# A three-pass fp32 encoder trunk with a seven-product block scheme on one core: six units instead of four lead each FFN, the second rows' squares move ahead of a weight conversion, and 276 GpSimd sums and products are issued on VectorE

## The chip, the cores and the metric

The kernel runs on one core of a Trainium2 chip. A core has five engines that run at the same time, each through its own queue of instructions in order: TensorE (PE in the profile; its weight loads are PEld), VectorE (DVE), ScalarE (ACT), GpSimd (POOL) and SyncE (SP), which here starts most of the transfers. They meet through semaphores. Matmuls write the accumulators in PSUM; everything else stands in SBUF. Times are device microseconds (us) of one execution. The kernel before was run three times: 2573.06, 2574.07 and 2575.15 us, median 2574.07.

## The reference, cut to what matters

One layer (DEPTH = 1) over 2048 frames of 1024 channels, all in fp32:

```python
xn = rmsnorm(x, norm1_g)
z = xn @ w_in                          # 4608 columns
u_pool, zq, zf, zi, zo, zg = split(z)  # 512 each, and 2048 of gates
gates = sigmoid(zg + b_gate)
ya = pool_mixer(u_pool, ...) @ w_pa    # running means over 2, 4, 8 and 16 frames
yb = hgrn2_mixer(zq, zf, zi, zo, ...) @ w_pb
x = x + (gates[0] * ya + gates[1] * yb) @ w_o
h = rmsnorm(x, norm2_g) @ w_up         # 2 * 2816 columns
val, gate = split(causal_conv3(h) + conv_b)
x = x + (silu(gate) * val) @ w_down
return rmsnorm(x, final_g)
```

## The kernel before, in words

**Products.** Each large matrix product is cut two by two, in rows (frames), in columns and in the contracted channels, and is made of seven smaller products P1 to P7 instead of eight, in Strassen's manner. For that the activations are needed in seven *forms*: the blocks B11, B21 and B22 as they are, and the combinations T1 to T4 (P1 takes B11, P2 B21, P6 T2, P5 T1, P7 T3, P4 T4, P3 B22). The weights are needed in seven forms as well: P1, P2 and P4 take a quarter of the weights as it is, P5, P6, P7 and P3 a sum of two to four quarters. Each operand is then split into a rounded part (`h`) and the remainder (`l`), and each product is three matmuls: high by high, high by low, low by high. The results of P1, P6, P7 and so on are joined through three PSUM banks, X (P1, P2), Z (P6, P7, P4) and V (P5, P3), with copies and differences `e1`, `u2` and `u3` between them: ScalarE copies X to `e1` after P1, VectorE makes `u2` after P6 and `u3` after P7, each from Z and `e1`, and Z is free for the next product after that.

**Two halves.** The program goes twice through the same stages, once for each 1024 frames (blocks 0 and 1, then 2 and 3, of 512 frames each). A half is: the io projection (`proj_io`, values `v` and output gates `z`; here the frames stand on the partitions, with four column blocks `j` of each bank), the mixer (`mixer`: 14 units in the order of PROJ, with the heads' recurrence and the pooling as tasks between them), the two branches `pa` and `pb`, the output rows `wo`, and the FFN (`ffn`: 22 `up` units, then the rows `dn`, then the last norm).

**The weight stream.** `Stream` loads 512-column quarters into a ring of eight places (`raw`) and converts them into a ring of six operands (`ops`), at most four ahead of the product that uses them: `convert` has ScalarE copy the rounded part (line 205) and VectorE subtract it for the remainder (line 206). Where an operand is a sum, its conversion first makes the sum: three for an io P3, two for P6, one each for P5 and P7 (line 338, `w24s0` and so on; one sum of P6 and one of P3 stand on VectorE, the other 20 in all on GpSimd), and four per unit of the other projections (`comb`, line 397, on GpSimd, 56). This happens in the first half only; sums are kept in DRAM and loaded by the second half. The sums for `up`, `wo` and `dn` are made by accumulating transfers ahead of their use.

**The forms.** `forms_a_task` makes B11 and B21 of the first block of a half, `forms_b_task` the rest from the second block. Both begin with the row norms (`row_rstd`: two squares per row tile on ScalarE, line 635; GpSimd's scalar work; the scaling, line 649). Block 1's rows come through the task `nxt[2]`, and in the first half its steps are taken when the planner's slots come. T4, and T3 of the FFN's input, are differences of two SBUF tiles (lines 746 and 729, on GpSimd). `add_forms` (line 1103) makes the forms of `y` for the branches and of the gated FFN result `g` for `dn`, 120 sums, on GpSimd. GpSimd also has products by sigmoids (lines 1137, 1212, 1420, 1484) and the sums of two of the four pooling windows (line 778).

**What sets the order.** A scheduler that simulates the program's timeline lays the instructions on the engines' queues; `behind`, `second` and `in_turn` add order that has no data in it. `up_order` fixes the order of the `up` units' products: P1 and P2 of the heads, which need only block 0's forms B11 and B21, stand first; the other five products of the heads follow, and then unit by unit. With N_HEADS = 2 the heads are units 0 to 3.

```python
heads = [(0, 1), (2, 3), (4, 5)][:N_HEADS]
res = [(m, p) for ms in heads for p in ("P1", "P2") for m in ms]
```

## Time and profile before

| | before |
|---|---|
| median of three runs | 2574.07 us (2573.06 to 2575.15) |
| the profiled execution | 2575.64 us, its span 2573.9 us |
| mean granted TensorE clock | 0.993 of full speed |
| TensorE busy | 2519.3 us, 98% |
| VectorE busy | 1964.0 us, 76%, 3382 instructions |
| ScalarE busy | 1191.9 us, 46% |
| GpSimd busy | 851.5 us, 33%, 1209 instructions |

The span runs from the first to the last instruction; the execution's own time has 1.7 us around it. In the rows of the profile, `out<-in` gives the tiles by the program's names with the numbers left out, `x4` is a count, and the brackets at the end hold the idle time of the engine just before and what ended it. A row of waits gives the waiting engine, tile and line, then the releasing one, and total, count and longest. A row of a stretch of time gives its length, then busy us and count of PE, PEld, DVE, ACT and POOL, then the granted clock, the transfers' share and GB/s.

### The profile page before, as it was taken

How to read it: one execution, taken by the hardware profiler on the slowest of the kernel's cores; microseconds unless marked ns; L12 is line 12 of the kernel's file. 1: busy time of each engine (PE TensorE's matmuls, PEld its weight loads, DVE VectorE, ACT ScalarE, POOL GpSimd, SP SyncE). 2: the span in 40 equal slices, each digit the busy share in tenths (PEclk: the TensorE clock that was granted, in tenths of full speed). 3: DMA queues.
4: the chain of work that ended last, by engine and by line, in shares of the span. 5: the costliest groups of instructions: out<-in, count | busy, mean ns of one | idle time of the engine just before them, and what ended most of it. 6: DMA issues, size and time to landing. Idle time of an engine off the chain costs nothing.

```text
span 2573.9 us, 35491 instructions
## 1 busy us (share of the span) xinstructions
PE 2519.3 (98%) x11464; PEld 2057.0 (80%) x11464; DVE 1964.0 (76%) x3382; ACT 1191.9 (46%) x2244; POOL 851.5 (33%) x1209
## 2 busy tenths in 40 slices
PE   7899999999999999999999999999999999999998
PEld 6678888788788888878878888888887888888887
DVE  7878788478789777786486776775978987778844
ACT  5335434324555544554364354442355554445533
POOL 6534344031445333462141111200223433334502
PEclk9899999999999999999999999999999999999999
DMA  6787768767788888887364343356442454446942
GB/s 219 254 248 204 210 201 247 215 223 245 179 235 235 235 242 230 252 318 252 107 211 149 99 139 119 120 160 224 143 165 88 151 153 144 144 139 209 366 149 98
DMA packets 254058, 496.88 MB, mean 193 GB/s; under 512 B 26736, under 2 KB 43248, under 8 KB 253552
## 3 DMA queue, kind: packets, MB, share of 16 engines
q1 hardware_dynamic: 187968, 319.89, 38.5%
q0 software_dynamic: 41504, 110.64, 16.8%
q10 hardware_dynamic: 24400, 64.08, 7.3%
q8 instruction: 90, 1.47, 0.2%
q14 instruction: 96, 0.79, 0.1%
HBM read 384.94 MB, written 187.17 MB: 222 GB/s over the span
## 4 chain that ended last, share of the span: by engine, by line
PE 89%; DVE 5%; issue 2%; ACT 2%; DMA 1%; POOL 1%; SPq 0%; DVEq 0%; POOLq 0%; ACTq 0%
PE dn_P L145 16%; PE up_Z L145 14%; PE up_V L145 9%; PE up_X L145 9%; PE wo_P L145 6%; PE gr_Z L145 5%; PE pb L145 3%; PE pa L145 3%; PE gr_X L145 3%; PE gr_V L145 3%; PE fr_Z L145 3%; PE fr_V L145 2%; PE fr_X L145 2%; PE pl L867 1%; PE io_Z L145 1%
## 5 line engine op out<-in xcount | busy, mean ns | idle before, releaser
L205 ACT CAST ops<-raw 128x512 fp32r<-128x512 f32 x732 | 452.7, 620 | 792.9 <-PE dn_P L145 147.6
L206 DVE TENSOR_TENSOR ops<-raw,ops 128x512 fp32r<-128x512 f32 x732 | 555.4, 762 | 207.8 <-ACT ops L205 204.0
L1409 DVE SCALAR_TENSOR_TENSOR e<-h,cols,e 128x512 f32<-128x512 f32 x176 | 142.4, 812 | 30.8 <-ACT e L1407 26.5
L1407 ACT ACTIVATE e<-h,cols 128x512 f32<-128x512 f32 x176 | 142.4, 814 | 29.1 <-DVE h L997 21.0
L1412 DVE SCALAR_TENSOR_TENSOR e<-h,cols,e 128x512 f32<-128x512 f32 x176 | 133.7, 768 | 2.8
L805 POOL DMA_DIRECT2D g_P<-dg_P x154 | 83.3, 543 | 101.3 <-PE dn_P L145 28.5
L1103 POOL TENSOR_TENSOR gf_P<-e,e 128x512 f32<-128x512 f32 x44 | 65.6, 1493 | 153.3 <-DVE e L1418 98.8
L1103 POOL TENSOR_TENSOR gf_P<-gf_P,e 128x512 f32<-128x512 f32 x44 | 59.1, 1344 | 66.6 <-DVE e L1418 66.1
L1402 POOL COPY h<-h 128x2 f32<-128x2 f32 x88 | 39.5, 463 | 121.2 <-DVE h L995 119.2
L1404 POOL COPY hist<-h 128x2 f32<-128x2 f32 x88 | 38.8, 442 | 121.1 <-DVE h L997 119.4
L1416 ACT ACTIVATE e<-e 128x512 f32<-128x512 f32 x88 | 55.6, 632 | 46.2 <-DVE e L1412 46.0
L997 DVE TENSOR_TENSOR h<-up_u,up_V 128x512 f32<-128x512 f32 x88 | 60.0, 682 | 13.3 <-PE up_V L145 12.8
L1212 POOL TENSOR_TENSOR q<-q,qs 128x512 f32<-128x512 f32 x16 | 22.7, 1419 | 139.0 <-ACT qs L1211 127.9
L854 POOL COPY qm<-q 128x64 f32<-128x64 f32 x64 | 24.4, 404 | 117.7 <-DVE q L860 43.9
L1079 DVE TENSOR_TENSOR x<-x,wo_P 128x512 f32<-128x512 f32 x88 | 56.0, 675 | 8.3 <-PE wo_P L145 8.1
L1249 ACT ACTIVATE gt<-gt,cols 128x512 f32<-128x512 f32 x48 | 34.8, 725 | 57.5 <-DVE gt L997 35.1
L1079 DVE TENSOR_TENSOR ac<-ac,dn_P 128x512 f32<-128x512 f32 x72 | 47.3, 682 | 18.4 <-PE dn_P L145 16.5
L1103 POOL TENSOR_TENSOR yf_P<-ya,ya 128x512 f32<-128x512 f32 x16 | 21.1, 1322 | 117.3 <-DVE ya L1326 117.3
L628 POOL TENSOR_SCALAR ro<-so 128x4 f32<-128x4 f32 x16 | 3.2, 199 | 156.8 <-ACT junk L969 156.8
L1477 POOL TENSOR_TENSOR fss<-fss 128x1 f32<-128x1 f32 x16 | 6.6, 415 | 144.2 <-ACT fo L1467 144.2
L1432 POOL DMA_DIRECT2D dg_P<-gf_P x88 | 50.1, 569 | 8.5 <-POOL gf_P L1103 7.7
L1031 ACT COPY up_e<-up_X 128x512 f32<-128x512 f32 x44 | 25.8, 586 | 57.6 <-PE up_X L145 47.5
(1267 smaller groups left out, 8303.4 us busy)
## 6 DMA issues: line engine op xcount, KB each, us to landing
g_P<-dg_P POOLq DMA_DIRECT2D x154, 256.0 KB, 6.4
raw<-in_w_up_t SPq DMA_DIRECT2D x132, 256.0 KB, 3.1
raw<-in_w_in_t SPq DMA_DIRECT2D x98, 256.0 KB, 3.2
dg_P<-gf_P POOLq DMA_DIRECT2D x88, 256.0 KB, 3.8
raw<-in_w_io SPq DMA_DIRECT2D x68, 256.0 KB, 4.8
dg_P<-e SPq DMA_DIRECT2D x66, 256.0 KB, 3.2
raw<-in_w_dn SPq DMA_DIRECT2D x66, 256.0 KB, 4.5
x<-in_x SPq DMA_DIRECT2D x64, 256.0 KB, 5.1
```

The source lines that it names most:

```text
L145: count[1] = pe.matmul(*args, **kw)
L205: self.mark = act.copy(hi, v)
L206: dve.tensor_tensor(lo, v, f32(hi), ALU.subtract)
L805: eng.dma_start(t, d)
L997: dve.tensor_tensor(dst, t, ps, ALU.add if how == "add" else ALU.subtract)
L1079: dve.tensor_tensor(t, t, ps[j], ALU.add if sg > 0 else ALU.subtract)
L1103: pin(pool.tensor_tensor(t, x0, x1, op))
L1407: in_turn(act.activation(t, h[:, 2:], AF.Identity, bias=col(o_cb + mt), scale=col(o_cw + 4 * MF + mt)))
L1409: in_turn(second(dve.scalar_tensor_tensor(t, h[:, 1 : 1 + TB], col(o_cw + 2 * MF + mt), t, ALU.mult, ALU.add)))
L1412: dve.scalar_tensor_tensor(t, h[:, 0:TB], col(o_cw + mt), t, ALU.mult, ALU.add)
L1416: in_turn(act.activation(g, g, AF.Silu))
L1432: pool.dma_start(d, t)
```

## The change

Three things are edited. N_HEADS goes from 2 to 3, so P1 and P2 of units 4 and 5 join the leading products of each FFN. Right after block 0's forms are written out, one step of block 1's task is taken, which emits its row norms, and the first weight conversion from number 6 on is put behind the last of its squares (`opening`). And every `tensor_tensor` of two whole tiles that stood on GpSimd is issued on VectorE: 276 of them. Lines of the changed kernel are two to four numbers higher.

```diff
-N_HEADS = 2
+N_HEADS = 3
-G_POOL = 4
...
             self.mark = act.copy(hi, v)
+            if j >= N_OPS and opening[0] is not None:
+                behind(self.mark, opening[0])
+                opening[0] = None
             dve.tensor_tensor(lo, v, f32(hi), ALU.subtract)
...
-                        (dve if i == (p == "P6") and p != "P5" and p != "P7" else pool
-                         ).tensor_tensor(t2, t, r.tile, ALU.add)
+                        dve.tensor_tensor(t2, t, r.tile, ALU.add)
...
-            pool.tensor_tensor(t, x0, x1, ALU.add)
+            dve.tensor_tensor(t, x0, x1, ALU.add)
...
-        heads = [(0, 1), (2, 3), (4, 5)][:N_HEADS]
+        heads = [(0, 1), (2, 3), (4, 5), (6, 7)][:N_HEADS]
...
-            act.activation(junk[hf], halves[hf], AF.Square, accum_out=ss[:, hf : hf + 1])
+            ins = act.activation(junk[hf], halves[hf], AF.Square, accum_out=ss[:, hf : hf + 1])
+            if name == "x1_3":
+                opening[0] = ins
...
-                pool.tensor_tensor(t, full["B11"][k], t2, ALU.subtract)
+                dve.tensor_tensor(t, full["B11"][k], t2, ALU.subtract)
...
-            pool.tensor_tensor(t4, full["B21"][k], full["T2"][k], ALU.subtract)
+            dve.tensor_tensor(t4, full["B21"][k], full["T2"][k], ALU.subtract)
...
-        add = pool if g % 2 == 0 else dve
-            add.tensor_tensor(t[:, a:528], s[:, a:528], s[:, a - k : 528 - k], ALU.add)
+            dve.tensor_tensor(t[:, a:528], s[:, a:528], s[:, a - k : 528 - k], ALU.add)
...
-            pin(pool.tensor_tensor(t, x0, x1, op))
+            pin(dve.tensor_tensor(t, x0, x1, op))
...
-            (dve if hf == 0 else pool).tensor_tensor(t, t, g, ALU.mult)
+            dve.tensor_tensor(t, t, g, ALU.mult)
...
-                    pool.tensor_tensor(t, t, g, ALU.mult)
+                    dve.tensor_tensor(t, t, g, ALU.mult)
...
-                    (pool if m < G_POOL else dve).tensor_tensor(g, g, ts[0, hf], ALU.mult)
+                    dve.tensor_tensor(g, g, ts[0, hf], ALU.mult)
...
-                    pool.tensor_tensor(res[c], res[c], fg[c], ALU.mult)
+                    dve.tensor_tensor(res[c], res[c], fg[c], ALU.mult)
...
     join(nxt[1])
+    nxt[2].step()
     Task(setup_task())
```

What it does to the queues is shown at three places. The rows are the instructions in the order in which they stand on one engine.

ScalarE at the program's start, before. `raw6` to `ops6` is the seventh weight conversion, the lines of 663 are block 0's forms, those of 635 the squares of block 1's row tiles 0 to 3, and 1142 the copies of bank X after P1 (`io_e`).

```order
L205 CAST ops6_427<-raw6_110 128x512
L663 ACTIVATE x0_b6_268<-x0_t6_138,cols_84 128x512
L205 CAST ops7_444<-raw7_112 128x512
L663 ACTIVATE x0_b7_274<-x0_t7_139,cols_84 128x512
L635 ACTIVATE x1_xs0_0_307,x1_0ss_309<-x1_0_0_216 128x512
L635 ACTIVATE x1_xs0_1_308,x1_0ss_309<-x1_0_1_218 128x512
...
L635 ACTIVATE x1_xs3_1_341,x1_3ss_342<-x1_3_1_230 128x512
L1142 COPY io0_e1_0_449<-io0_X_0_290 128x512
L1142 COPY io0_e1_1_454<-io0_X_1_291 128x512
```

The same place with the change (lines 667, 637, 204 and 1145 are the same statements).

```order
L667 ACTIVATE x0_b6_268<-x0_t6_138,cols_84 128x512
L667 ACTIVATE x0_b7_274<-x0_t7_139,cols_84 128x512
L637 ACTIVATE x1_xs0_0_280,x1_0ss_282<-x1_0_0_216 128x512
L637 ACTIVATE x1_xs0_1_281,x1_0ss_282<-x1_0_1_218 128x512
...
L637 ACTIVATE x1_xs3_1_314,x1_3ss_315<-x1_3_1_230 128x512
L204 CAST ops6_427<-raw6_110 128x512
L204 CAST ops7_444<-raw7_112 128x512
L1145 COPY io0_e1_0_449<-io0_X_0_334 128x512
L1145 COPY io0_e1_1_454<-io0_X_1_335 128x512
```

Conversions 6 and 7 have moved from between block 0's last forms to behind the eight squares, right ahead of the copies.

VectorE toward the end of the io projection, before: `io0_u3` is read from bank Z after P7, `z0_1` is the output gate, `w24s0` the first of the three sums for the operand of conversion 24. The second and third sums (`w24s1`, `w24s2`) and the products of `z0_1` by their sigmoids stand on GpSimd.

```order
L1148 TENSOR_TENSOR io0_u3_3_1070<-io0_Z_3_710,io0_e1_3_470 128x512
L997 TENSOR_TENSOR z0_1_0_1072<-io0_u3_0_1055,io0_V_0_843 128x512
...
L997 TENSOR_TENSOR z0_1_3_1090<-io0_u3_3_1070,io0_V_3_846 128x512
L338 TENSOR_TENSOR w24s0_1099<-raw40_903,raw41_905 128x512
L338 TENSOR_TENSOR w25s0_1130<-raw44_962,raw45_999 128x512
L206 TENSOR_TENSOR ops24_1106<-w24s2_1103,ops24_1106 128x512
L338 TENSOR_TENSOR w26s0_1161<-raw48_1109,raw49_1111 128x512
L206 TENSOR_TENSOR ops25_1137<-w25s2_1134,ops25_1137 128x512
```

The same place with the change.

```order
L1151 TENSOR_TENSOR io0_u3_3_1070<-io0_Z_3_710,io0_e1_3_470 128x512
...
L1140 TENSOR_TENSOR z0_1_1_1078<-z0_1_1_1078,zs0_1_1_1079 128x512
L1000 TENSOR_TENSOR z0_1_3_1090<-io0_u3_3_1070,io0_V_3_846 128x512
L1140 TENSOR_TENSOR z0_1_2_1084<-z0_1_2_1084,zs0_1_2_1085 128x512
L340 TENSOR_TENSOR w24s0_1099<-raw40_903,raw41_905 128x512
L1140 TENSOR_TENSOR z0_1_3_1090<-z0_1_3_1090,zs0_1_3_1091 128x512
L340 TENSOR_TENSOR w24s1_1101<-w24s0_1099,raw42_934 128x512
L340 TENSOR_TENSOR w24s2_1103<-w24s1_1101,raw43_936 128x512
L340 TENSOR_TENSOR w25s0_1130<-raw44_962,raw45_999 128x512
L208 TENSOR_TENSOR ops24_1106<-w24s2_1103,ops24_1106 128x512
```

Between `io0_u3_3` and the remainder `ops24` there are now thirteen instructions instead of six: the four products and the chain `w24s0` to `w24s2` stand in VectorE's own queue, with two sums for the next operand among them.

ScalarE in the opening of the first FFN, before. `m1_T23h`, `m1_T10h` and so on are the rounded parts of the forms T2, T1 and T3, `h0_2` and `h0_3` the P2 results of units 2 and 3, `ops185` a weight conversion.

```order
L606 CAST m1_T23h_6787<-m1_t23_6783 128x512
L991 COPY h0_2_0_0_6794<-up0_2_X_6649 128x512
L606 CAST m1_T10h_6805<-m1_t10_6690 128x512
L991 COPY h0_3_0_0_6818<-up0_3_X_6669 128x512
L205 CAST ops185_6876<-raw171_6616 128x512
L606 CAST m1_T11h_6855<-m1_t11_6718 128x512
L205 CAST ops186_6895<-raw172_6635 128x512
L606 CAST m1_T12h_6864<-m1_t12_6753 128x512
```

The same place with the change.

```order
L608 CAST m1_T23h_6787<-m1_t23_6783 128x512
L204 CAST ops185_6867<-raw171_6616 128x512
L994 COPY h0_2_0_0_6794<-up0_2_X_6649 128x512
L608 CAST m1_T10h_6805<-m1_t10_6690 128x512
L994 COPY h0_3_0_0_6818<-up0_3_X_6669 128x512
L1034 COPY up0_4_e1_6838<-up0_4_X_6820 128x512
L608 CAST m1_T11h_6855<-m1_t11_6718 128x512
L204 CAST ops186_6887<-raw172_6635 128x512
L1034 COPY up0_5_e1_6862<-up0_5_X_6840 128x512
L994 COPY h0_4_0_0_6882<-up0_4_X_6820 128x512
L994 COPY h0_5_0_0_6901<-up0_5_X_6840 128x512
L608 CAST m1_T12h_6912<-m1_t12_6753 128x512
```

Four copies of units 4 and 5 (`up0_4_e1`, `up0_5_e1`, `h0_4`, `h0_5`) and their conversions stand among the casts of T1, all of them behind the last cast of T2, `m1_T23h`. On TensorE the groups of matmuls are the same; P1 and P2 of units 4 and 5 stand ahead of the first P6.

More of the change, by code (lines that the diff above doesn't have):

```diff
@@ L235, in tile_trunk @@
     urgent = [None]
+    opening = [None]
     def first(ins):
```

## The prediction, made blind

> **What bounds the kernel now.** I read the page first, then TensorE's waits, then the same work in the two halves of the program side by side, then the engines' timelines at the places found.
>
> ```profile
> span 2573.9 us, 35491 instructions
> ...
> PE 2519.3 (98%) x11464; PEld 2057.0 (80%) x11464; DVE 1964.0 (76%) x3382; ACT 1191.9 (46%) x2244; POOL 851.5 (33%) x1209
> ...
> PE 89%; DVE 5%; issue 2%; ACT 2%; DMA 1%; POOL 1%; SPq 0%; DVEq 0%; POOLq 0%; ACTq 0%
> ```
>
> TensorE is busy 98% of the span and carries 89% of the chain that ended last. The change touches no product, so all it can win is TensorE's idle time, 2573.9 - 2519.3 = 54.6 us, and time at a reduced clock. TensorE's own waits say where (total, times, longest, in us):
>
> ```profile
> PE x_t L655 <- DVE x_xs L649: 8.8, 2, 7.8
> PE fr_Z L145 <- DVE ops L206: 4.5, 1, 4.5
> PE io_Z L145 <- DVE io_u L1148: 4.3, 1, 4.3
> PE io_X L145 <- ACT io_e L1142: 3.5, 2, 3.0
> PE gr_Z L145 <- DVE gr_u L1033: 3.3, 2, 2.4
> PE up_Z L145 <- ACT m_T23h L606: 2.6, 2, 1.3
> PE up_Z L145 <- DVE m_T23l L607: 2.3, 2, 1.1
> PE up_Z L145 <- DVE up_u L1037: 2.2, 4, 0.6
> PE io_Z L145 <- DVE x_t L712: 2.1, 2, 1.8
> ```
>
> The 7.8 us is the program's first wait, for the first input rows; the change leaves it. The others lie in three places. In the next view (busy us and count by engine, clock, DMA share, GB/s) the first two rows are the io projection of the first and of the second half, the next two the rest of the mixer up to `pb`, then the openings of the two FFNs, then the rest of the first FFN's `up`:
>
> ```profile
> 16.90:113.70 96.80, 86.27 (x361) 68.83 (x362) 80.60 (x104) 43.17 (x84) 60.92 (x76) 0.93 0.65 219
> 1312.50:1395.20 82.70, 81.90 (x369) 66.60 (x370) 68.25 (x101) 44.52 (x86) 21.92 (x24) 1.00 0.48 158
> 113.70:524.30 410.60, 399.67 (x1977) 331.62 (x1976) 316.46 (x707) 167.16 (x368) 143.04 (x150) 0.99 0.76 220
> 1395.20:1787.60 392.40, 391.23 (x1970) 328.00 (x1969) 270.37 (x693) 166.60 (x363) 47.84 (x80) 1.00 0.44 139
> 650.70:712.00 61.30, 55.87 (x244) 43.40 (x244) 50.45 (x71) 33.27 (x63) 27.13 (x34) 0.97 0.77 188
> 1913.20:1974.50 61.30, 57.04 (x249) 44.53 (x248) 48.56 (x69) 34.26 (x63) 21.47 (x28) 0.97 0.28 87
> 712.00:1085.00 373.00, 373.00 (x1615) 302.73 (x1614) 305.54 (x429) 186.23 (x292) 156.91 (x224) 1.00 0.87 237
> ```
>
> The two halves multiply the same, but only the first makes the weights' sums (the second loads them). The first io pass is 14.1 us longer, the first mixer pass 18.2. An `up` opening idles 61.30 - 55.87 = 5.4 us, the second 4.3; the steady `up` idles not at all. Some waits also cost clock:
>
> ```profile
> 33.90:37.30 3.40, 3.40 (x10) 2.65 (x9) 2.40 (x2) 0.88 (x3) 3.17 (x7) 0.50 0.89 285
> 88.50:95.30 6.80, 5.22 (x12) 4.13 (x13) 6.80 (x12) 2.46 (x4) 2.17 (x2) 0.50 0.06 20
> 122.60:129.50 6.90, 5.02 (x12) 3.96 (x13) 4.58 (x9) 0.35 (x1) 0.00 (x0) 0.51 1.05 354
> 464.00:467.40 3.40, 3.40 (x10) 2.62 (x9) 2.52 (x5) 1.75 (x4) 0.00 (x0) 0.50 0.43 131
> 682.40:685.80 3.40, 3.40 (x9) 2.63 (x8) 3.39 (x2) 1.14 (x2) 3.40 (x4) 0.50 0.64 90
> 1945.30:1948.80 3.50, 3.50 (x11) 2.68 (x10) 2.88 (x3) 0.76 (x2) 3.50 (x3) 0.51 0.24 76
> ```
>
> After each of the long waits, and after the FFN openings' pairs of about 1.2 us, the granted clock is half; half of TensorE's busy time there is lost: 1.7, 2.6, 2.5, 1.7, 1.7 and 1.7 us. The account closes: the first io pass has 96.80 - 86.27 = 10.5 us of idling and 1.7 + 2.6 of clock, 14.8, for its 14.1.
>
> [...]
>
> **Part 1: the second rows' squares in front.** In the start, ScalarE waits 6.69 us for TensorE before the cast `ops6`, with the squares of block 1's rows queued behind it; they run 27.13 to 32.03 and hold up the copies `io_e`, for which TensorE waits:
>
> ```profile
> 24.93 0.62 ACT L205 CAST ops<-raw 128x512 fp32r<-128x512 f32 x1 [6.69 <-PE io_X L145]
> 27.13 0.63 ACT L635 ACTIVATE x_xs<-x 128x512 f32<-128x512 f32 x1
> 32.03 2.01 ACT L1142 COPY io_e<-io_X 128x512 f32<-128x512 f32 x4
> 32.74 0.71 PE L145 MATMUL io_X<-ops,x_f4h 128*128 128x512 f32 x2 [3.00 <-ACT io_e L1142]
> ```
>
> The new order puts the eight squares (4.9 us) into that hole of 6.69 us. The copies then follow the end of P1, 32.74 - 3.00 = 29.74, within one copy (2.01 / 4 = 0.5 us): 2.5 us of the wait goes, and its clock, 1.7. Block 1's forms start some 7 us earlier, so the waits for `x_xs` (8.8 - 7.8 = 1.0) and `x_t` (1.8) should shrink: I take 1.3 of 2.8. Gain **5.5**, bounds 3 and 2.5 + 1.7 + 2.8 = 7.
>
> **Part 2: 276 sums and products from GpSimd to VectorE.** By the code: 20 io sums, 56 of the other projections, 24 of the forms' differences, 16 pooling sums, 120 in the forms of `g` and `y`, 40 products. The same statement stood on both engines, which gives the price directly:
>
> ```profile
> L1420 DVE TENSOR_TENSOR e<-e,e 128x512 f32<-128x512 f32 x36 | 24.7, 686 | 0.6
> L1420 POOL TENSOR_TENSOR e<-e,e 128x512 f32<-128x512 f32 x8 | 10.6, 1327 | 24.9 <-ACT e L1416 24.9
> ```
>
> A sum lasts 0.69 us instead of 1.33, and a row of them advances by 2.47 / 4 = 0.62 us (the row at 89.26 below). So VectorE takes on 276 x 0.62 = 171 us of work. What it gives back is blocked time:
>
> ```profile
> 682.81 4.26 POOL L746 TENSOR_TENSOR m_t<-m_b,m_t 128x512 f32<-128x512 f32 x3
> 683.08 4.55 DVE L206 TENSOR_TENSOR ops<-raw,ops 128x512 fp32r<-128x512 f32 x1
> ...
> 75.28 6.88 POOL L746 TENSOR_TENSOR x_t<-x_b,x_t 128x512 f32<-128x512 f32 x4
> 89.26 2.47 DVE L1148 TENSOR_TENSOR io_u<-io_Z,io_e 128x512 f32<-128x512 f32 x4
> 93.13 5.92 POOL L1137 TENSOR_TENSOR z<-z,zs 128x512 f32<-128x512 f32 x4 [10.97 <-ACT zs L1136]
> 99.01 2.67 POOL L338 TENSOR_TENSOR w24s<-w24s,raw 128x512 f32<-128x512 f32 x2
> 101.71 0.62 ACT L205 CAST ops<-w24s 128x512 fp32r<-128x512 f32 x1 [6.88 <-POOL w24s L338]
> 102.36 1.12 DVE L206 TENSOR_TENSOR ops<-w24s,ops 128x512 fp32r<-128x512 f32 x1 [5.70 <-ACT ops L205]
> 113.30 1.31 DVE L206 TENSOR_TENSOR ops<-w27s,ops 128x512 fp32r<-128x512 f32 x1
> ```
>
> One VectorE subtraction with both inputs in SBUF lasted 4.55 us beside three GpSimd sums of 4.26; both engines crawl. The two mixer passes size it: the first has 56 sums more on GpSimd, and VectorE is busy 316.46 - 270.37 = 46.1 us longer, of which 14 more instructions explain 8.7. The other 37.4 / 56 = 0.67 us per sum is blocking. A moved sum costs VectorE 0.62 and frees 0.67: its load stays where it was. The gain is that a chain of sums gets twice as short.
>
> *The io pass.* From `io0_u3_0` to the last sum-made operand `ops27` VectorE needed 113.30 - 89.26 = 24.0 us; the new order has 30 instructions there, 30 x 0.62 = 18.6, against 4 + 3 products of 12 matmuls at 373.00 / 1615 = 0.231 us each in four column blocks, 7 x 2.77 = 19.4 us, on TensorE. So TensorE, not VectorE, should set the pace. To be won are 4.3, its clock 2.6 and some 0.9 of small waits, 7.8. The loads of four raw quarters for each of these operands stay, so I take **4.5**. Below: were nothing freed, 28 x 0.62 = 17.4 would join 80.60, 98 us in a stretch of 96.80, and 2 us would be lost.
>
> *The first mixer pass.* It opens with the 4.5 us for `ops` (clock 2.5), behind the `z` products of both engines; I take 5.5 of 7.0. Of the 2.4 us at 461 and its clock, 1.7, I take 2, and 1 goes back to new short waits: **6.5**, bounds 0 and 14 (all its idling, 10.9, and clock, 4.2, less the 1.2 that the second pass keeps).
>
> *Elsewhere* sums join VectorE where TensorE does not idle (`up`: 305.54 busy of 373.00, plus 48 x 0.62 = 30 if nothing is freed, still 336; the 16 `yf` sums at the end of `pb`). Cover is TensorE's own 373.00 of 373.00; were it gone in `pb`, 16 x 0.62 = 10 us would show. I put **-2**, bounds -6 and +2.
>
> **Part 3: six units lead.** P1 and P2 of units 4 and 5 now stand before the first use of the T2 forms: 4 x 12 x 0.231 = 11.1 us. The waits for `m_T23h`, `m_T23l` and the like are together under 5.4 us in an opening, so they go; so does the clock, 1.7 each. The waits on `up_u` (2.2, four times) stay, and a third pair adds two in each half, 1.1 in all. Gain 5.4 + 4.3 + 3.4 - 2.2 - 1.1 = **9.8**. ScalarE pays four more copies before the T1 casts; VectorE makes the T3 and T4 forms without the 4.55 us block. Bounds: 6 if half of it comes back at P7 to P4, 12 if `up_u` goes too.
>
> [...]
>
> **The sum.** 5.5 + 4.5 + 6.5 - 2 + 9.8 = 24.3. The profiled execution took 2575.64 us, so 2551.3; the median of the runs, 2574.07, lies 1.6 below that execution: **2550**.
>
> **Rivals.**
> - *The loads take over.* The raw ring has eight places, and an io P3 operand needs four; if landing sets the pace, the io pass and `fr_Z` keep their waits: 4.5 + 4 less, 2558. For it: 0.65 of the DMA share is used there already. Against: 101.71 waited 6.88 us for a sum, not for a load. 0.12.
> - *The lead only moves the wait.* The forms are late by VectorE's queue, and two more units' work delays them too: 2560. Against: the extra work before them is four ScalarE copies. 0.08.
> - *Nothing measurable*: the freed time is no more than the taken, and gaps reappear elsewhere: 2573. 0.05.
> - *Slower: the sums block the u2/u3 subtractions.* In a mixer unit TensorE comes back to the Z bank one product, 2.77 us, after VectorE may read it; four instructions ahead in VectorE's queue are enough to stop it. Each of 14 units now has four sums in that queue. If nothing were freed, the pass would hold 316.46 + 72 x 0.62 = 361 of 410 us, and if all 56 sums fell on the path, 34.7 us would be added and part 2's 9 not won: 2575 + 35 - 15 = 2595. It decides from the point where over half the sums stand between a product's end and its subtraction. Against: in the new order most stand after u2 or u3, and 0.67 is freed for each. 0.06.
>
> **How the numbers follow.** The forecast has 0.69; its own range is 2540 to 2560. All lower bounds together give 1 us, all upper 43; ends on both sides at two thirds and the first two rivals give 2536 to 2566. A measurement of this kernel tells 0.2%, 5 us. Faster: the forecast, the first two rivals, less a little for their tails, 0.88; same 0.06; slower 0.06.
>
> **What would show it.** The io pass nearer 85 us than 97, without half clock at 33 and 88; no wait of `io_X` for `io_e` over 1 us; the first mixer pass near 404; the openings with under 2 us of idling and full clock; VectorE busy within 25 us of 1964, GpSimd under 500; `ops` differences near 0.69 us. Wrong if TensorE's idling stays over 45 us, or shows waits for `gr_u` or `fr_u` beyond 8 us in sum.

## The result, and the profile after

The changed kernel took 2553.2 us (median of four runs, 2552.64 to 2555.24), the kernel before on the same chip 2574.19. The ratio is 0.992, 95% interval 0.9903 to 0.9937: 20.6 us less, between 16 and 25. On a second chip the ratio was 0.9922 (0.9908 to 0.9936). The forecast was 2550, range 2536 to 2566.

The page of the changed kernel, its first lines:

```profile
span 2553.4 us, 35421 instructions
...
PE 2513.3 (98%) x11464; PEld 2053.4 (80%) x11464; DVE 1969.0 (77%) x3658; ACT 1191.2 (47%) x2244; POOL 460.1 (18%) x933
```

VectorE has taken 276 instructions more and is busy 1969.0 us against 1964.0: the load stayed where it was, as the prediction had it. GpSimd fell from 851.5 to 460.1. TensorE idles 40.1 us instead of 54.6 (this counts the start, before its first operand) and is busy 6.0 us less for the same products, 3.5 us of it time that was lost at half clock (nine stretches of 3.4 us before, which cost 13.6 us, six now, which cost 10.1).

TensorE's waits now:

```profile
PE io_Z L144 <- DVE io_u L1151: 4.0, 1, 4.0
...
PE up_Z L144 <- ACT m_T43h L608: 2.3, 2, 1.2
PE up_Z L144 <- ACT m_T42h L608: 2.3, 2, 1.2
PE gr_X L144 <- ACT gr_e L1034: 1.8, 1, 1.8
PE io_Z L144 <- DVE x_t L716: 1.5, 1, 1.5
PE fr_Z L144 <- ACT ops L204: 1.4, 1, 1.4
...
PE up_Z L144 <- DVE up_u L1040: 1.2, 2, 0.6
...
PE io_X L144 <- ACT io_e L1145: 0.3, 1, 0.3
```

`io_e` is down to 0.3 us, `m_T23h`, `m_T23l` and `gr_u` are gone, and the 4.5 us for the first `fr_Z` are 1.4. But `io_u` still stops TensorE for 4.0 us, and in both FFN openings T42 and T43, for which nothing waited over 0.24 us before, hold it up twice for 1.2 us.

The same by stages (busy us and count by engine, clock, DMA share, GB/s). First three rows of the kernel before that were not shown yet: the first `up`, the first `dn`, the second `up`.

```profile
650.70:1085.20 434.50, 429.07 (x1857) 346.29 (x1857) 356.20 (x499) 219.60 (x355) 184.05 (x258) 1.00 0.85 230
1085.20:1312.50 227.30, 224.02 (x981) 181.02 (x979) 151.17 (x231) 116.82 (x225) 84.49 (x146) 1.00 0.68 232
1913.20:2346.70 433.50, 429.24 (x1857) 346.42 (x1856) 355.28 (x499) 219.52 (x355) 154.91 (x236) 1.00 0.45 141
```

The changed kernel: the first io stage, the mixer up to `pb`, the first `up`, the first `dn`, the second `up`.

```profile
17.40:107.80 90.40, 83.76 (x360) 67.04 (x361) 77.97 (x131) 42.78 (x82) 20.73 (x47) 0.96 0.67 230
107.80:507.60 399.80, 395.02 (x1978) 328.97 (x1978) 312.07 (x781) 168.70 (x370) 46.34 (x78) 1.00 0.78 227
633.90:1066.60 432.70, 429.54 (x1857) 347.21 (x1856) 361.76 (x554) 220.10 (x358) 109.08 (x209) 0.99 0.85 232
1066.60:1291.70 225.10, 223.67 (x982) 181.18 (x980) 146.11 (x236) 113.50 (x220) 66.75 (x133) 1.00 0.67 232
1892.90:2326.40 433.50, 430.12 (x1857) 347.32 (x1856) 362.46 (x554) 219.81 (x358) 80.49 (x185) 0.99 0.45 142
```

| stage | before | after | difference | forecast |
|---|---|---|---|---|
| first io | 96.8 | 90.4 | -6.4 | -10.0 (parts 1 and 2) |
| first mixer, to `pb` | 410.6 | 399.8 | -10.8 | -6.5 |
| first `up` | 434.5 | 432.7 | -1.8 | -5.5 (of part 3's 9.8) |
| second `up` | 433.5 | 433.5 | 0.0 | -4.3 (the rest of 9.8) |
| first `dn` | 227.3 | 225.1 | -2.2 | +2 for all of "elsewhere" |

So the total came within 4 us of the forecast with terms that missed on both sides: the mixer gave 4 us more than forecast, the two `up` stages 8 us less.

### The profile page after: what moved, and what is told of

Read it like the earlier page. It is cut to its first block, busy times and chain, and to the rows that moved or that the text cites. A ratio compares the mean times of both kernels' runs of the same rounds, so it can differ in the third digit from the quotient of the medians.

```text
span 2553.4 us, 35421 instructions
## 1 busy us (share of the span) xinstructions
PE 2513.3 (98%) x11464; PEld 2053.4 (80%) x11464; DVE 1969.0 (77%) x3658; ACT 1191.2 (47%) x2244; POOL 460.1 (18%) x933
## 3 DMA queue, kind: packets, MB, share of 16 engines
q8 instruction: 90, 1.47, 0.2%
## 4 chain that ended last, share of the span: by engine, by line
PE 56%; ACT 1%; DVE 0%; issue 0%; POOL 0%; DVEq 0%; POOLq 0%; ACTq 0%
PE dn_P L144 16%; PE up_Z L144 7%; PE up_X L144 5%; PE up_V L144 5%; PE wo_P L144 3%; PE gr_Z L144 3%; PE gr_X L144 2%; PE pb L144 2%; PE pa L144 2%; PE gr_V L144 2%; PE io_Z L144 1%; PE fr_Z L144 1%; PE fr_X L144 1%; PE io_V L144 1%; PE fr_V L144 1%; PE pl L870 1%
## 5 line engine op out<-in xcount | busy, mean ns | idle before, releaser
L208 DVE TENSOR_TENSOR ops<-raw,ops 128x512 fp32r<-128x512 f32 x732 | 501.5, 688 | 202.0 <-ACT ops L204 197.7
L1412 DVE SCALAR_TENSOR_TENSOR e<-h,cols,e 128x512 f32<-128x512 f32 x176 | 131.0, 748 | 33.5 <-ACT e L1410 26.0
L1415 DVE SCALAR_TENSOR_TENSOR e<-h,cols,e 128x512 f32<-128x512 f32 x176 | 131.4, 747 | 2.5
L1000 DVE TENSOR_TENSOR h<-up_u,up_V 128x512 f32<-128x512 f32 x88 | 60.0, 682 | 10.8 <-PE up_V L144 10.7
L1252 ACT ACTIVATE gt<-gt,cols 128x512 f32<-128x512 f32 x48 | 34.8, 725 | 54.6 <-DVE gt L1000 35.9
L1405 POOL COPY h<-hist 128x2 f32<-128x2 f32 x88 | 32.4, 413 | 95.8 <-issue 48.2
L870 PE MATMUL pl<-qm,k 128*128 128x192 f32 x256 | 45.2, 326 | 0.0
L870 PEld LDWEIGHTS pl<-qm,k 128*128 128x128 f32 x256 | 42.7, 190 | 1.9
L998 DVE TENSOR_TENSOR h<-up_Z,up_e 128x512 f32<-128x512 f32 x44 | 30.3, 689 | 15.0 <-PE up_Z L144 14.5
L144 PE MATMUL up_Z<-m_T43h,ops 128*128 128x512 f32 x88 | 36.3, 412 | 2.3 <-ACT m_T43h L608 2.3
```

The costliest lines, as they stand in the source:

```text
L144: count[1] = pe.matmul(*args, **kw)
L208: dve.tensor_tensor(lo, v, f32(hi), ALU.subtract)
L870: pe.matmul(pa_[:, c * 192 : c * 192 + 192], ks[:, (i + c) * P : (i + c + 1) * P], mv[:, c].rearrange("p s x -> p (s x)"), start=True, sto ...
L1000: dve.tensor_tensor(dst, t, ps, ALU.add if how == "add" else ALU.subtract)
L1405: pool.tensor_copy(h[:, 0:2], hist[:, mt] if hf == 0 else hs[s, 0][:, TB : TB + 2])
L1412: in_turn(second(dve.scalar_tensor_tensor(t, h[:, 1 : 1 + TB], col(o_cw + 2 * MF + mt), t, ALU.mult, ALU.add)))
```

## The experiments

All ratios are to the kernel before on the same chip, and differences between kernels are differences of their ratios, 0.001 for 2.57 us. The changed kernel is taken at 0.9922, from its second set (`after_again`, 2553.02 us).

> The changed kernel itself, so that the kernels beside it can be compared on one chip. Nothing new: 0.992 of the kernel before, about 2553 us where the kernel before takes 2574.

### What the lead is worth: `two_heads` and `all_back`

`two_heads` takes the lead back, `all_back` all 276 moved instructions.

```diff
-N_HEADS = 3
+N_HEADS = 2
```

> The changed kernel with N_HEADS = 2 again; the early squares and all 276 moved sums stay. By part 3 of the prediction the lead of six units is worth 9.8 us, so this kernel takes 2553.2 + 9.8 = 2563 us. By the profile of the changed kernel the `up` stages became only 1.7 and 0.0 us shorter, since the waits for T2 and T1 were replaced by waits for T4 (two of 1.2 us in each opening) with 3.4 us of clock behind them. If that is what the lead brings (it moves the wait), this kernel takes about 2555. A third way: on VectorE's queue the T3 and T4 differences make the T2 and T1 forms later than they were in the kernel before, and without the lead both openings idle more than before (over 5.4 us each): 2565 or more; then the small net gain hides two large terms of opposite signs.

> The changed kernel with all 276 sums and products on the engines where they stood before; the early squares and the lead of six units stay. By part 2 of the prediction the move is worth 4.5 + 6.5 - 2 = 9 us: 2562 us. By the stages of the two profiles it is worth more in the mixer (10.9 us) and less in the io stage (6.4 - 5.4 = 1.0 us), and the first `dn` gains 2.3: 14 us, 2567 us, provided that the openings of the two FFNs stay as they are. If instead GpSimd makes the T4 forms early enough, the lead has its full worth here, the two openings become 5 us shorter each, and the sum is about 2557.

`two_heads`: 2557.28 us, 0.9930 (0.9918 to 0.9942), 2 us above the changed kernel and not the 9.8 of the forecast. Its `up` stages:

```profile
633.90:1067.70 433.80, 428.72 (x1858) 346.33 (x1857) 362.71 (x554) 220.31 (x356) 106.25 (x208) 1.00 0.86 232
1893.50:2327.80 434.30, 429.20 (x1857) 346.43 (x1856) 364.52 (x554) 220.90 (x358) 77.51 (x185) 1.00 0.47 142
```

They are 1.1 and 0.8 us longer than with the lead. Its waits:

```profile
PE up_Z L144 <- ACT m_T43h L608: 2.4, 2, 1.2
PE up_Z L144 <- ACT m_T42h L608: 2.3, 2, 1.2
PE up_Z L144 <- DVE up_u L1040: 2.1, 4, 0.6
...
PE up_Z L144 <- ACT m_T23h L608: 1.4, 2, 0.7
...
PE up_V L144 <- DVE m_T12l L609: 0.6, 2, 0.3
...
PE up_Z L144 <- DVE m_T23l L609: 0.5, 2, 0.2
```

TensorE waits for T42 and T43 as long as with the lead (4.7 us here, 4.6 there): the lead neither brings these waits nor hides them. What it takes away are the waits for T2 and T1, and the move of the sums had already cut those, from 4.0 and 2.8 us in the two openings of the kernel before to 1.2 in each. With the lead the `up` stages idle 1.9 and 1.7 us less (3.2 and 3.4 instead of 5.1 and 5.1), but have two stretches at half clock each instead of one, which takes 0.8 and 0.9 us back.

The third way of the expectation (over 5.4 us of idling per opening) did not happen: the stages idle 5.1 us.

`all_back`: 2561.04 us, 0.9943 (0.9931 to 0.9955). The mixer up to `pb` and the two `up` stages:

```profile
111.70:517.60 405.90, 396.50 (x1978) 330.04 (x1977) 314.80 (x707) 167.22 (x368) 144.19 (x150) 1.00 0.78 222
644.60:1073.50 428.90, 427.15 (x1857) 345.50 (x1857) 363.74 (x499) 218.27 (x355) 184.17 (x258) 1.00 0.87 233
1902.40:2331.80 429.40, 427.64 (x1857) 345.32 (x1856) 360.51 (x499) 218.26 (x355) 159.12 (x236) 1.00 0.47 142
```

With the sums on GpSimd the same lead makes the `up` stages 434.5 - 428.9 = 5.6 and 433.5 - 429.4 = 4.1 us shorter than before, 9.7 together, at full clock throughout: the 9.8 of part 3. It is the move of part 2 that takes 3.8 and 4.1 of them away again. The whole move is worth 0.9943 - 0.9922, 5.4 us, for which the forecast had 9. By its time alone (0.9943 of 2574.07 is 2559.4 us) the run lies between the first of the expected ways, 2562, and the last, 2557; the stages show the last.

### Which of the moved instructions cost the openings: `forms_back`

```diff
-                dve.tensor_tensor(t, full["B11"][k], t2, ALU.subtract)
+                pool.tensor_tensor(t, full["B11"][k], t2, ALU.subtract)
...
-            dve.tensor_tensor(t4, full["B21"][k], full["T2"][k], ALU.subtract)
+            pool.tensor_tensor(t4, full["B21"][k], full["T2"][k], ALU.subtract)
```

> The changed kernel with only the 24 differences that make T3 (of the FFN's input) and T4 on GpSimd again. Theory: the two `up` stages were 428.9 and 429.4 us with everything on GpSimd and the same lead, and 432.8 and 433.5 in the changed kernel; the T4 differences on VectorE alone make that step, since there they stand behind `u3` and the last remainder, while GpSimd makes them ahead. Then both stages fall to about 429 us, and this kernel takes 8 us less than the changed one, 0.9889 of the kernel before. Rival: the other sums on VectorE are what crowds the opening, or the blocked subtractions (one took 4.55 us beside three T4 differences) give back what is won: within 2 us of the changed kernel.

2544.85 us, 0.9890 (0.9877 to 0.9904): 8.2 us below the changed kernel, as the theory had it. The `up` stages:

```profile
630.60:1059.00 428.40, 426.58 (x1858) 345.38 (x1857) 364.70 (x547) 220.23 (x358) 123.03 (x218) 1.00 0.87 235
1885.20:2314.00 428.80, 427.04 (x1857) 345.31 (x1856) 364.21 (x546) 219.81 (x358) 95.21 (x193) 1.00 0.47 144
```

24 of the 276 instructions are a loss of 8 us on VectorE; the other 252 are a gain of 13 to 14 (`all_back` against this run). In the first io stage, too, TensorE waits only 0.5 us for `io_u` here, against 4.0 in the changed kernel. VectorE's queue in the opening of the changed kernel shows why:

```profile
686.33 0.69 DVE L609 TENSOR_TENSOR m_T41l<-m_t,m_T41h 128x512 fp32r<-128x512 f32 x1
686.94 0.68 DVE L609 TENSOR_TENSOR m_B221l<-m_b,m_B221h 128x512 fp32r<-128x512 f32 x1
687.54 0.68 DVE L1040 TENSOR_TENSOR up_u<-up_Z,up_e 128x512 f32<-128x512 f32 x1
688.50 0.69 DVE L208 TENSOR_TENSOR ops<-raw,ops 128x512 fp32r<-128x512 f32 x1 [0.28 <-ACT ops L204]
689.11 0.68 DVE L1000 TENSOR_TENSOR h<-up_u,up_V 128x512 f32<-128x512 f32 x1
689.71 0.69 DVE L750 TENSOR_TENSOR m_t<-m_b,m_t 128x512 f32<-128x512 f32 x1
691.13 0.69 DVE L609 TENSOR_TENSOR m_T42l<-m_t,m_T42h 128x512 fp32r<-128x512 f32 x1 [0.74 <-ACT m_T42h L608]
691.74 0.68 DVE L609 TENSOR_TENSOR m_B222l<-m_b,m_B222h 128x512 fp32r<-128x512 f32 x1
692.35 0.68 DVE L750 TENSOR_TENSOR m_t<-m_b,m_t 128x512 f32<-128x512 f32 x1
```

The difference for T42 (689.71) stands behind `u3` of unit 0 and the row after it, then ScalarE casts, VectorE waits 0.74 us for the cast, and only behind the B222 remainder comes the next difference: one turn of this chain is 692.35 - 689.71 = 2.64 us, while TensorE uses up a T4 form in 3 x 0.23 = 0.7. In the kernel before, GpSimd made three of the four differences in one go from 682.81 on (its row stands in the prediction), 17 us ahead of the first P4. GpSimd took 1.42 us a difference (4.26 for the three) where VectorE takes 0.69, and was ahead all the same: a second queue had the differences ready before VectorE came to them.

### The forms in another order: `t4_ahead` and `b22_last`

`b22_last` casts the four B22 forms after all T4 forms (and, in the first io stage, after `u3` has been issued). `t4_ahead` does that and also issues the four T4 differences before the T1 casts, on VectorE.

```diff
+        t4 = []
+        for k in range(4):
+            while len(full["B21"]) <= k:
+                yield 4
+            t4.append(slot(f"{name}t4{k}"))
+            dve.tensor_tensor(t4[k], full["B21"][k], full["T2"][k], ALU.subtract)
         for k in range(4):
             forms["T1"].append(split(t1[k], f"{name}T1{k}"))
             yield 5
...
-            dve.tensor_tensor(t4, full["B21"][k], full["T2"][k], ALU.subtract)
-            forms["T4"].append(split(t4, f"{name}T4{k}"))
-            forms["B22"].append(split(b22[k], f"{name}B22{k}"))
+            forms["T4"].append(split(t4[k], f"{name}T4{k}"))
+            yield 1
+        while src[0] == "x" and not u3_made[0]:
+            yield 1
+        for k in range(4):
+            forms["B22"].append(split(b22[k], f"{name}B22{k}"))
             yield 1
```

> The changed kernel with one difference in the making of the forms: the four T4 differences are issued before the T1 casts, the four B22 forms after all T4 forms, and in the first io stage the B22 forms wait until `u3` has been issued. Theory: on VectorE the T4 differences and their casts form a chain (difference, cast on ScalarE, remainder, next difference) with the B22 remainders between them, and that is why P4 waits for T42 and T43 in both openings (2.3 + 0.5 us and 3.4 us of clock each) and why `u3` of the io stage comes 4.0 us late, with 1.7 us of clock. Then the openings gain about 5 us each and the io stage 2.4 (four remainders at 0.62) to 4: 2553.2 - 13 = 2540 us, range 2536 to 2545. Rival: VectorE as a whole is behind at these places, so whatever is put first makes something else late (B22 for P3, or u3): within 3 us of 2553.

> The changed kernel with only the second half of the reordering of the forms: the four B22 forms after all T4 forms (and after `u3` in the first io stage), the T4 differences where they were. If the B22 remainders in VectorE's queue are what delays T42, T43 and `u3`, this has the whole gain: 0.985 of the kernel before, 2537 us. If the chain of difference, cast, remainder and next difference behind `u3` is what P4 waits for, the openings keep their waits of 1.2 us, and only `u3` of the io stage gains: 2549 us, 0.990.

`t4_ahead`: 2536.47 us, 0.9851 (0.9836 to 0.9866), 18 us below the changed kernel and 38 below the kernel before, the fastest of this study and at the low end of the range expected. The first io stage and the two `up` stages:

```profile
16.90:103.20 86.30, 83.13 (x361) 67.06 (x362) 78.19 (x132) 43.24 (x83) 20.64 (x47) 0.96 0.73 248
628.30:1054.80 426.50, 426.50 (x1857) 345.72 (x1856) 361.60 (x555) 220.24 (x358) 112.08 (x211) 1.00 0.88 236
1880.60:2306.70 426.10, 426.10 (x1858) 345.63 (x1857) 361.58 (x555) 219.59 (x358) 83.66 (x185) 1.00 0.47 145
```

TensorE is busy in the `up` stages from end to end; the openings idle not at all. No wait for `io_u` is left in the io stage. VectorE does the same work (78.19 us there, 77.97 in the changed kernel), so the rival, that VectorE as a whole is behind, falls: it was the order in its queue.

`b22_last`: 2543.85 us, 0.9881 (0.9868 to 0.9895), between the two numbers of its expectation. The wait for `io_u` goes from 4.0 to 1.2 us by the B22 remainders alone; in each opening a wait of 0.6 us for T43 is left, with shorter ones for T42, and in the first one of 0.9 for B22. Both edits act: 10.6 us for the B22 forms, 7.7 more for the differences.

With this order the lead shows its worth again. `t4_ahead_two_heads` is `t4_ahead` with N_HEADS = 2:

> The kernel with the T4 differences ahead and the B22 forms last, with N_HEADS = 2. The lead was worth 0.95 and 0.83 us in the two openings as long as the T4 differences stood late on VectorE, and 5.6 and 4.1 with them on GpSimd. If the lead and the T4 forms are two limits one behind the other, each hiding the other, the lead shows its worth here: the `up` stages are 431 to 433 us instead of 426.6 and 426.0, 0.988 of the kernel before. If the T4 forms alone were the limit, within 2 us of the kernel with six units: 0.985 to 0.986.

2541.78 us, 0.9872 (0.9856 to 0.9887), 5.4 us above `t4_ahead`; the `up` stages last 429.2 and 428.5 us. That is less than the 431 to 433 expected and more than "T4 alone" allowed. In each opening TensorE waits 0.9 us for T2, as in `two_heads`, and 1.2 us for T1, where `two_heads` had 0.3; probably the T1 forms come later because the T4 differences now stand ahead of their casts. T2 and T4 do not hide one another: the waits for T2 are the same whether T4 is late or not, and those for T4 the same with and without the lead.

### The early squares: `squares_only`, `no_early_squares`, `t4_ahead_no_squares`

`squares_only` adds these lines, with the mark on the last square, to the kernel before; `no_early_squares` and `t4_ahead_no_squares` take them out of the changed kernel and of `t4_ahead`.

```diff
+            if j >= N_OPS and opening[0] is not None:
+                behind(self.mark, opening[0])
+                opening[0] = None
...
+    nxt[2].step()
```

> The kernel before with part 1 alone: block 1's squares early, the seventh weight conversion behind them. By the prediction 5.5 us less, 0.9979 of the kernel before. By the profile with everything on GpSimd again (part 1 and the lead) the io stage was 94.7 us against 96.8: the 3.0 us for `io_e` were gone, but up to the first P6 the waits for the T2 forms were 3.3 us instead of 2.7, with half a clock window more there. So the forms of block 1 take the place of the copies, and part 1 alone is worth about 2 us: 0.9992. It would be 3.7 if the clock windows fall well.

> The changed kernel without the early step of block 1's task and without the order behind its squares. Theory (part 1): TensorE waits for `io_e` again, 3.0 us, and loses 1.7 us of clock behind it, and the waits for block 1's forms grow by 0.7 us: 2553.2 + 5.4 = 2558.6 us, all of it in the io stage, which goes from 90.4 to about 96 us. Rival: with the sums on VectorE the start of the io stage is ruled by VectorE's queue, and what the squares win is waited for again at P6 or P7: within 1 us of 2553.2.

> The kernel with the T4 differences ahead and the B22 forms last, without part 1. If part 1 is worth its 5.5 us of the prediction, 2542 us where the same kernel with part 1 takes 2536.5 (0.9851 to 0.987 of the kernel before). If it is worth 2 us, 0.9859. If the waits only change places (3.0 for `io_e` against 2.0 for T2 and 1 us of a later start), no difference: 0.985.

`squares_only`, the kernel before with part 1 alone, took 2572.25 us over 11 runs, 0.9994 (0.9985 to 1.0003): 1.5 us, which is not to be told from nothing, and below the 5.5 of the forecast. `no_early_squares` was 0.9929 (0.9916 to 0.9942), 1.8 us above the changed kernel; `t4_ahead_no_squares` 0.9864 (0.9850 to 0.9877), 3.3 above `t4_ahead`. The three agree on 1.5 to 3.3, though none is clear of noise by itself: the first interval holds 1, and the other two overlap with those of the kernels that they are set against. The profile of `squares_only` is of its longest execution (2575.72 us), that of `no_early_squares` of one of 2554.23, 3 us under its median. In `squares_only` the 3.0 us for `io_e` are indeed gone, and these rows of TensorE in its start show where they went (transposes of block 1, each with the wait ahead of it):

```profile
39.12 0.76 PE L661 MATMUL x_t<-ident,x_xs 128*128 128x128 f32 x2 [1.62 <-DVE x_xs L655]
46.69 0.66 PE L661 MATMUL x_t<-ident,x_xs 128*128 128x128 f32 x4 [0.67 <-DVE x_t L718]
47.95 0.66 PE L661 MATMUL x_t<-ident,x_xs 128*128 128x128 f32 x4 [0.60 <-DVE x_t L718]
```

With the 1.5 us right behind them these waits sum to 4.4 us, where the kernel before waited 0.9 + 1.8 = 2.7. Block 1's rows and forms are made on VectorE, whose work did not become less. TensorE comes to block 1's transposes 3.9 us earlier (36.7 against 40.6), but to the first P6 behind them only 2.3 us earlier (50.1 against 52.3). The half clock moved too: one stretch at 33.9 in the kernel before, two from 49.0 on here (the mean granted clock of the io stage is 0.93 there and 0.95 here). In the changed kernel the waits for the forms are 2.0 us (0.5 and 1.5). By the profile without the early squares the start has the old shape again, 3.0 us for `io_e` and 1.4 for the forms, and the whole program is as long within 2 us.

### The sums one group at a time: `unit_sums_back` and `io_back`

`unit_sums_back` puts only line 399 (`comb`, 56 sums of the mixer's units) back on GpSimd, `io_back` only the 20 io sums and 8 products of `z`.

```diff
-            dve.tensor_tensor(t, x0, x1, ALU.add)
+            pool.tensor_tensor(t, x0, x1, ALU.add)
             tmp[key] = t
```

```diff
-                        dve.tensor_tensor(t2, t, r.tile, ALU.add)
+                        (dve if i == (p == "P6") and p != "P5" and p != "P7" else pool
+                         ).tensor_tensor(t2, t, r.tile, ALU.add)
...
-            dve.tensor_tensor(t, t, g, ALU.mult)
+            (dve if hf == 0 else pool).tensor_tensor(t, t, g, ALU.mult)
```

> The changed kernel with only the 56 weight sums of the mixer's units on GpSimd again. The first mixer pass up to `pa` was 356.7 us in the kernel before, 352.0 with everything on GpSimd again, 345.8 in the changed kernel. If these 56 sums are what the pass gains, it goes back to 352 us, and the kernel takes 6 us more than the changed one. By the waits of those profiles only the waits of the recurrence (`pl` 2.2 us) and of `gr_Z` (2.5 us, less the 1.8 that the changed kernel waits for `gr_e`) are theirs, the rest (the 4.4 us for the first `fr_Z` with the clock behind it) belongs to the io sums: then the pass takes about 348.7 us, 3 us more. VectorE's busy time in the pass should be lower by no more than 5 us, since 56 sums of 0.62 leave and 0.67 us of blocking for each comes back.

> The changed kernel with the 20 io sums and the 8 products of `z` on GpSimd again. If the chain of sums for the last io operands is what the first `fr_Z` waits for, that wait is 4.4 us again (1.4 in the changed kernel) with a half-clock stretch behind it, the io stage takes 93 to 95 us (90.4), and the kernel takes 6 to 8 us more than the changed one. If the loads of the raw quarters set that pace, within 1.5 us of it.

`unit_sums_back`: 2557.37 us, 0.9946 (0.9933 to 0.9959), 6.2 us above the changed kernel: the first expectation. The mixer up to `pb`:

```profile
107.40:513.00 405.60, 398.48 (x1977) 331.19 (x1977) 318.48 (x725) 167.70 (x370) 123.27 (x134) 0.99 0.77 223
```

TensorE's waits for the first `fr_Z`:

```profile
PE fr_Z L144 <- DVE ops L208: 2.7, 1, 2.7
PE fr_Z L144 <- ACT ops L204: 2.1, 1, 2.1
```

VectorE's timeline at that place, and behind it GpSimd's:

```profile
109.68 2.88 DVE L1140 TENSOR_TENSOR z<-z,zs 128x512 f32<-128x512 f32 x2
113.09 2.86 DVE L1140 TENSOR_TENSOR z<-z,zs 128x512 f32<-128x512 f32 x2
```

```profile
110.27 1.74 POOL L399 TENSOR_TENSOR w31s<-raw,raw 128x512 f32<-128x512 f32 x1
111.97 1.71 POOL L399 TENSOR_TENSOR w34s<-w29s,raw 128x512 f32<-128x512 f32 x1
```

The waits for the first `fr_Z`, 4.8 us with 10.2 us at half clock behind them (some 4 us lost in this profile, which is of an execution of 2562.0 us; how much of it the runs of 2557 lost is open), are thus those of the unit sums: VectorE's pairs of products last 2.9 us beside GpSimd's sums, where a pair lasts 1.28 without them (at 108.98 in the changed kernel), and the remainders of the operands stand behind them in the queue. The assignment to the io sums in the expectation was wrong. The price per sum can be read off: VectorE is busy 318.48 - 312.07 = 6.4 us longer with 56 sums less, so for each sum on GpSimd its other work lasts (6.4 + 56 x 0.62) / 56 = 0.73 us longer; the prediction had 0.67.

`io_back`: 2556.92 us, 0.9935 (0.9922 to 0.9949), 3.3 us above the changed kernel. Its io stage, 16.40 to 109.10, lasts 92.7 us instead of 90.4, and the first `fr_Z` waits 1.2 us, not the expected 4.4. Neither number of the expectation came, not 6 to 8 and not under 1.5. The io sums are worth some 3 us and act within the io stage: the intervals of the two ratios overlap, but on this chip each of the five runs is longer than all four of the changed kernel.

## Why the prediction was right, and where its terms were not

**Part 1, 5.5 us: mis-sized.** Measured 1.5 to 3.3, not clear of noise. The step that failed is "block 1's forms start some 7 us earlier, so the waits for `x_xs` and `x_t` should shrink": from the kernel before to `squares_only` they grew from 2.7 to 4.4 us, and from the kernel without the early squares to the changed one from 1.4 to 2.0. The squares do start 7.8 us earlier (19.4 instead of 27.1), but of the 3.9 us that TensorE comes earlier to block 1's transposes in `squares_only`, the first P6 behind them keeps 2.3. The 1.7 us of clock were not safe either: in `squares_only` half clock came back behind these waits, and `no_early_squares` lost none behind its 3.0 us. I counted the wait that goes and not the next one.

**Part 2, the load: right.** "A moved sum costs VectorE 0.62 and frees 0.67" became 0.73 freed, and VectorE's busy time moved by 5 us for 276 instructions. The rival in which the sums block the `u2` and `u3` subtractions did not occur; the waits for `gr_u`, 3.3 us before, are gone in one profile of the changed kernel and 1.7 in the other.

**Part 2, the io stage, 4.5: 3.3 by `io_back`, but not by the way it was argued.** "TensorE, not VectorE, should set the pace" was worked out from `io0_u3_0` on. What TensorE waited for was `u3` itself, whose place is behind the T4 and B22 forms in VectorE's queue, and that stayed at 4.0 us. `t4_ahead` shows the wait gone when those forms stand elsewhere. Of the rival *The loads take over* there is a trace here: ahead of `u3` VectorE waits 0.4 and 1.2 us for raw quarters (at 64.6 and 66.5), so part of the 4.0 may be theirs, which no run separates. `t4_ahead` has 0.9 us of that wait and none of TensorE's.

**Part 2, the mixer, 6.5: the mechanism right, the stage gave 10.8.** The unit sums are worth 6.2 by `unit_sums_back`. The other 4.7 are not theirs: `all_back`, with every sum on GpSimd, has them too (405.9 against 410.6). There TensorE is busy 399.67 - 396.50 = 3.2 us less for the same products, two stretches at half clock fewer (the last section shows behind what idling they came). No term of the sum foresaw this part; as far as the runs show it is luck.

**Part 2, "elsewhere", -2: the step that failed.** I put the 24 form differences among the sums that "join VectorE where TensorE does not idle" and, in part 3, wrote that VectorE makes the T3 and T4 forms "without the 4.55 us block". I priced the block that goes and not the place in the queue that each difference gets. It costs 8.2 us (`forms_back`). `dn` gave 2 us instead of costing any.

**Part 3, 9.8: right by itself, 9.7 measured (`all_back`), 2 as it stands in this kernel.** The rival "the lead only moves the wait", with its chance of 0.08, looks as if it had happened, but did not: the waits for T42 and T43 are there without the lead as well (`two_heads`), and in `all_back`, with the copies of two more units, no wait for T2 or T1 is left. It was part 2 that left the lead less to win and put the T4 differences where TensorE waits for them.

**The total.** Of the 24.3 forecast, 20.6 came. Too much was put down for part 1 (3), the io stage (1.2) and the openings (8), too little for the mixer's clock (4.7) and for `dn` and the rest (2 gained where 2 were to be lost): 24.3 - 12.2 + 8.7 = 20.8. That the total came so near the forecast is luck in good part: terms 12.2 us too high and 8.7 too low nearly cancel.

**What should show it.** Held: `io_e` without a wait over 1 us, VectorE within 25 us of 1964, GpSimd under 500, the `ops` differences (mean 0.69 us), the mixer near 404 (399.8), full clock at 33, TensorE's idling under 45 us (40.1), and by a hair the io stage (90.4, where the middle between 85 and 97 is 91). Not held: full clock at 88 (a half-clock stretch stands at 86), the openings under 2 us of idling at full clock (3.2 us, and clock lost).

## What to carry to other kernels

When an instruction is moved to a faster engine, price its place in that engine's queue as well as its duration: 24 differences that ran in under half the time (0.69 us instead of 1.47 to 1.84) cost 8 us, since on the slower engine they had run ahead and now stood behind the work they did not depend on. When a wait is removed, look up what the same engine needs next and who makes it, before the gain is booked. Where a queue is full, what it holds need not shrink: putting forms in the order in which they are used was worth 18 us with no instruction less.

## What the runs showed of the hardware

**The half clock came in multiples of 3.41 us, and not behind the longest wait alone.** In the profiles of the kernel before and of the changed kernel the granted clock changes at times that are whole multiples of 3.413 us apart (in the kernel before: 33.9, 88.5, 122.6, 464.0, 682.4; 54.6 us, for example, is 16 of them). I laid this spacing over TensorE's busy time. From the first record of the clock on, and leaving out the program's end, all nine stretches at full clock that held 2.1 us of idling or more were followed by one at half clock (2.40, 2.27, 2.72, 2.60, 2.37 and 2.11 us before, 2.78, 2.11 and 2.18 after); of the eleven with 0.95 to 1.46 us, none was; of the five with 1.58 to 1.90, two (those with 1.68 and 1.82). Two other runs show a wait of 3.0 us without loss of clock and shorter ones with it. The kernel without the early squares, around its 3.0 us for `io_e`:

```profile
25.80:29.20 3.40, 1.96 (x9) 1.28 (x7) 2.85 (x5) 3.40 (x12) 3.40 (x9) 1.00 0.43 140
29.20:32.60 3.40, 1.84 (x8) 1.56 (x9) 1.39 (x5) 3.40 (x10) 3.08 (x13) 1.00 0.94 308
32.60:36.00 3.40, 3.40 (x17) 2.76 (x16) 2.39 (x6) 0.50 (x1) 3.08 (x8) 1.00 0.88 277
```

The wait falls across two stretches, 1.4 and 1.6 us of idling, and the clock stays at 1.00. And `t4_ahead`, two waits of 0.5 and 1.5 us within one:

```profile
43.60:47.00 3.40, 1.41 (x9) 0.96 (x8) 3.27 (x5) 1.23 (x3) 0.00 (x0) 1.00 0.41 149
47.00:50.40 3.40, 3.40 (x10) 2.62 (x9) 3.29 (x6) 1.18 (x2) 0.00 (x0) 0.51 0.30 77
```

2.0 us of idling, and the next stretch runs at half clock, 1.7 us lost. Two profiles of the changed kernel differ by about such a step: its io stage lasted 90.4 us at a mean clock of 0.96 in one and 88.8 us at 0.98 in the other (`after_again`).

**VectorE beside GpSimd's sums.** In `unit_sums_back` two `z` products on VectorE, which read two tiles in SBUF, lasted 2.88 and 2.86 us a pair beside GpSimd's sums (at 109.68 and 113.09), against 1.28 without them (at 108.98 in the changed kernel). The operation between the two pairs (`z<-io_Z,io_e` at 112.48), which reads bank Z, lasted 0.68 us beside the same sums, and 0.68 without them. But over the stage VectorE's other work lasts only 0.73 us longer for a sum, of the 1.36 that the sum itself takes (median of the 56 in the kernel before). Probably VectorE's other operations and its own waits fall into the same time; no run here separates them.
